# Sorting the experts ahead of the first unit, an earlier sum and an earlier overflow loop in a decoder layer with 32 experts

## The chip, the cores and the metric

One core of a Trainium2 chip runs the whole layer as one program. The metric is the device time of one execution in microseconds (us). A run is timed three times, and one more execution is recorded by the hardware profiler. The engines are named as in the profile: PE is TensorE, DVE is VectorE, ACT is ScalarE, POOL is GpSimd and SP is SyncE, which here issues the weight loads.

## The reference

One layer for one sequence of 512 tokens and a model width of 1024, in float32. A first half mixes tokens (HGRN2 and NSA attention). The second half, which the change touches, is a mixture of 32 experts: each token goes to its top 2 experts inside one group, each expert is a SwiGLU of width 512, and the two outputs are added with weights. A residual sum and a layer norm close the layer. Cut to that half:

```python
def _hier_moe(h, ...):
    ...
    comb = grp_p * jax.nn.softmax(top_l, axis=-1)
    expert = grp_idx * EXP_PER_GROUP + top_i
    ...
    order = jnp.argsort(e_flat)
    ...
    def expert_block(args):
        xb, e = args
        return (jax.nn.silu(xb @ w1[e]) * (xb @ w3[e])) @ w2[e]
    ...
    y = y_pad[dest] * w_s[:, None].astype(x.dtype)
    out = jnp.zeros_like(x).at[tok_s].add(y)

# in reference():
        y = (1 + g2[:, None]) * _hier_moe(h, ...)
        x = _layer_norm(ALPHA * x + y) * ln2_g[l] + ln2_b[l]
```

## The kernel before, in words

The program is written by hand as one list of instructions for each engine; an engine runs its list in order, and semaphores make it wait for the others. So the order of the code is the order on each engine.

The expert half works through 13 *units* (`units = [-2, -1] + ORDER`). A unit is 128 rows of gathered tokens, split among 1 expert of 128 rows, 2 of 64 or 4 of 32. Units -2 and -1 are the experts 0 to 3, which are known ahead of time. The other experts are ranked by their number of tokens, and a unit takes experts by rank: `sort_experts` counts the tokens (four matmuls on PE into `pcnt`), ranks the experts and works out each token's place on DVE, and leaves the order as integers in `ovi`. SP reads expert numbers from `ovi` (`ev`) to address the loads of the units after -1.

For each unit the code does, in this order: `weighted` (DVE: one-hot rows of the unit's tokens times their weights, `pw`); `up` (PE: the products p1 and p3 with exp_w1 and exp_w3; ACT: silu of p1; DVE: `s = silu(p1) * p3`); the loads of the next unit (`load_unit`, SP, tiles `ew` of 512 KB each, three matrices of four tiles for each expert); `combine` of the *previous* unit, whose weighted halves `yh` and `yl` are spread to the tokens by one-hot matmuls (PE, into `pcb`) and added to `acc` (DVE); for every second unit `gather` (PE, `pgx`) of the tokens of the next two; and `down` (PE: transposes `pat` and `ptw`, product `py` with exp_w2; DVE and ACT: `pT`, `y`, `yh`, `yl`). `todo` keeps what `combine` needs one unit later.

The weight tiles come from a ring of 36 buffers (`Q`), 24 of which are free for weights, so a load waits until PE has read the tile that was in its buffer. Other scratch of half that size comes from a ring of 24 buffers (`S`), PSUM from a ring of 8 (`PS`).

The last unit is taken apart. Its exp_w2 is loaded in quarters of 256 columns, its `down` is done by quarter (`quarter_up`, `quarter_y`), and `quarter_add` adds, for each quarter and each 128 tokens, the second to last unit's two terms and the last unit's two terms in one PSUM sum, and adds that to `acc` with a row sum for the norm. Ahead of the last quarter's sums stands `overflow()`, a loop over blocks of tokens beyond a unit's room; its number of turns is read at run time, and it is nought in the profiled execution. The four 128-row pieces are then normed and stored.

Of the kernel before, what the change touches and what calls it, by code (L numbers as in the profile page):

```python
# [21 lines left out]
F32 = mybir.dt.float32  # L22
F32R = mybir.dt.float32r
BF = mybir.dt.bfloat16
# [7 lines left out]
NT = T // 128  # L32
# [109 lines left out]
def hybrid_kernel(ctx, tc, a, out, dbg=None, stop=None):  # L142
# [17 lines left out]
    def S(name, dt=F32):  # L160
        return big.tile([128, 512], dt, name=name, tag="S", bufs=24)
# [1209 lines left out]
    def sort_experts():  # L1371

        pcnt = PS("pcnt")
        for j in range(NT):
            mm(pcnt[:, 0:32], onesb, mb[:, j, :], j == 0, j == NT - 1)
        srt = S("srt")
        key, rk, base, cap_, t6, cnt = (srt[:, 32 * j:32 * j + 32] for j in range(6))
        V.tensor_copy(cnt, pcnt[:, 0:32])
        V.scalar_tensor_tensor(key, cnt, 32.0, iota[:, 0:32], op0=OP.mult, op1=OP.subtract)
        V.tensor_scalar(key[:, 0:4], iota[:, 0:4], -1.0, -100.0, op0=OP.mult, op1=OP.add)  # L1380
        big2 = S("cmpm").bitcast(BF).rearrange("p (e f) -> p e f", e=32)
        V.tensor_tensor(big2, key[:, None, :].to_broadcast([128, 32, 32]),
                        key.rearrange("p (e o) -> p e o", o=1).to_broadcast([128, 32, 32]), op=OP.is_gt)
        V.tensor_reduce(rk.rearrange("p (e o) -> p e o", o=1), big2, axis=AX.X, op=OP.add)

        V.tensor_tensor(big2, rk[:, None, :].to_broadcast([128, 32, 32]),
                        iota[:, 0:32].rearrange("p (e o) -> p e o", o=1).to_broadcast([128, 32, 32]), op=OP.is_equal)
        V.tensor_tensor(big2, big2, iota[:, None, 0:32].to_broadcast([128, 32, 32]), op=OP.mult)
        V.tensor_reduce(ovf[:, 0:32].rearrange("p (j o) -> p j o", o=1), big2, axis=AX.X, op=OP.add)
        V.tensor_copy(ovi[:, 0:32], ovf[:, 0:32])  # L1390
        t1 = S("t1")[:, :256].rearrange("p (c i e) -> p c i e", c=2, i=NT)

        def look(dst, table):

            V.tensor_tensor(t1, oh2, table[:, None, None, :].to_broadcast([128, 2, NT, 32]), op=OP.mult)
            V.tensor_reduce(dst.rearrange("p c (i o) -> p c i o", o=1), t1, axis=AX.X, op=OP.add)

        V.tensor_scalar(cap_, rk, 2.0, 64.0, op0=OP.is_lt, op1=OP.mult)
        V.tensor_scalar(t6, rk, 12.0, 32.0, op0=OP.is_lt, op1=OP.mult)
        V.tensor_add(cap_, cap_, t6)
        V.tensor_scalar(t6, rk, 28.0, 32.0, op0=OP.is_ge, op1=OP.mult)
        V.scalar_tensor_tensor(cap_, cap_, 32.0, t6, op0=OP.add, op1=OP.add)
        V.tensor_scalar(base, rk, 64.0, 128.0, op0=OP.mult, op1=OP.add)
        V.scalar_tensor_tensor(base, rk, 128.0, base, op0=OP.mult, op1=OP.min)
        V.tensor_scalar(t6, rk, 32.0, 512.0, op0=OP.mult, op1=OP.add)
        V.tensor_tensor(base, base, t6, op=OP.min)
        look(bst, base)  # L1410
        look(capt, cap_)
        V.tensor_tensor(far, pos, capt, op=OP.is_ge)
        V.tensor_add(slots, bst, pos)
        V.scalar_tensor_tensor(slots, far, 1e5, slots, op0=OP.mult, op1=OP.add)
        probe("slots", slots)


        ov = S("ov")
        need, incl, st0, t5 = ov[:, 0:32], ov[:, 32:64], ov[:, 64:96], ov[:, 96:128]
        V.tensor_sub(t5, cnt, cap_)  # L1420
        V.tensor_scalar(need, t5, 0.0, None, op0=OP.is_gt)
        for j in range(1, 4):
            V.scalar_tensor_tensor(need, t5, 128.0 * j, need, op0=OP.is_gt, op1=OP.add)
        V.tensor_tensor_scan(incl, need, need, 0.0, OP.add, OP.max)
        V.tensor_sub(st0, incl, need)
        look(ob, st0)
        V.scalar_tensor_tensor(oslots, ob, 128.0, pos, op0=OP.mult, op1=OP.add)
        V.tensor_sub(oslots, oslots, capt)
        V.tensor_scalar(far, far, 1e5, -1e5, op0=OP.mult, op1=OP.add)
        V.tensor_add(oslots, oslots, far)  # L1430
        le = S("le").bitcast(BF)[:, 0:NOV * 32].rearrange("p (j e) -> p j e", j=NOV)
        V.tensor_tensor(le, incl[:, None, :].to_broadcast([128, NOV, 32]),
                        iota[:, 0:NOV].rearrange("p (j o) -> p j o", o=1).to_broadcast([128, NOV, 32]), op=OP.is_le)
        V.tensor_copy(ovf[:, 32:33], incl[:, 31:32])
        V.tensor_reduce(ovf[:, 33:33 + NOV].rearrange("p (j o) -> p j o", o=1), le, axis=AX.X, op=OP.add)
        V.tensor_copy(ovi[:, 32:33 + NOV], ovf[:, 32:33 + NOV])
# [21 lines left out]
        t = w[k // 2]  # L1458
        return t[k % 2] if isinstance(t, list) else t[:, (k % 2) * 512:(k % 2 + 1) * 512]

    def up(xe, n0, ws, rhs=k1):
        lhs = lambda k: xe[k // 2][:, k % 2, :]
        p1 = PS("p1")
        unit_mm(p1, lhs, n0, ws["exp_w1"], rhs, 8)
        s1 = S("s1")
        A.activation(s1, p1, AF.Silu)
        p3 = PS("p3")
        unit_mm(p3, lhs, n0, ws["exp_w3"], rhs, 8)
        V.tensor_mul(s1, s1, p3)  # L1469
        return s1  # L1470
# [50 lines left out]
    def overflow():  # L1521
        ocnt = cp.tile([128, 1], F32, name="ocnt")
        V.memset(ocnt, 0.0)
        nonlocal S
        S, s_ring = (lambda name, dt=F32: Q(name, dt)[:, 0:512]), S
        with tc.For_i(0, nblk, 1) as jb:
            ex = nc.sync.value_load(ovi[0:1, ds(jb + 33, 1)], min_val=0, max_val=NE - 1)
            rel = rel_to(oslots, ocnt)
            V.tensor_scalar(ocnt, ocnt, 128.0, None, op0=OP.add)
            pw = weighted(rel)  # L1530
            xe = gather(one_hots([rel]))

            ow = [S("ow") for _ in range(2)]

            def stream(name):

                def get(k):
                    w = ow[k % 2]
                    nc.sync.dma_start(w, expert_rows(name, ex)[:, k * 512:(k + 1) * 512])
                    return w  # L1540
                return get
            act = up(xe, 0, {n: [stream(n)] for n in ("exp_w1", "exp_w3")}, lambda w, k: w(k))
            combine(*down(act, {"exp_w2": [stream("exp_w2")]}, pw, lambda w, h: w(h)))

            for i in range(NT):
                V.tensor_reduce(sums[:, i, 0:3], acc[i][:, 0:768].rearrange("p (q n) -> p q n", q=3), axis=AX.X, op=OP.add)
                squares(i, 0)
        S = s_ring


    units = [-2, -1] + ORDER
    todo, hots, nblk = None, None, None
    ws = w_first
    for n, u in enumerate(units):
        pw = weighted(rels.pop(u))
        nxt = units[n + 1:n + 3] if n % 2 == 1 else []
        if nxt:
            for x in nxt:
                rels[x] = rel_to(slots, 128.0 * x)
            hots = one_hots([rels[x] for x in nxt])  # L1560
        if n == 4:

            nblk = nc.values_load_multi_w_load_instructions(
                ovi[0:1, 32:33], min_val=0, max_val=NOV - 1,
                skip_runtime_bounds_check_because="a sum of fewer blocks than NOV")[1][0]
        act = up(xe, (n % 2) * 128, ws)
        if n == 0:
            sort_experts()
        w_now = ws
        if n + 1 < len(units):  # L1570
            v_ = units[n + 1]
            if v_ < 0:
                es = (2, 3)
            elif v_ < 2:
                es = (ev(v_),)
            elif v_ < 7:
                es = (ev(2 * v_ - 2), ev(2 * v_ - 1))
            else:
                es = tuple(ev(4 * v_ - 16 + x) for x in range(4))
            ws = load_unit(es, quarters=n + 2 == len(units))  # L1580
        if todo is not None and n + 1 < len(units):
            combine(*todo)
        if nxt:
            xe = gather(hots)
        if n + 1 < len(units):
            todo = down(act, w_now, pw)
    l2g = row_bc("l2g", a["ln2_g"])
    l2b = row_bc("l2b", a["ln2_b"])

# [22 lines left out]

    def quarter_add(q, y, i):

        o = q % 2 * 256
        terms = [(todo[0], t[:, o:o + 256]) for t in todo[1][q // 2]] + [(pT, t) for t in y]
        pc_ = PS("pcb")[:, 0:256]
        for j, (p_, t) in enumerate(terms):
            mm(pc_, p_[:, i * 128:(i + 1) * 128], t, j == 0, j == 3)
        z = acc[i][:, q * 256:(q + 1) * 256]  # L1620
        V.tensor_tensor_reduce(out=z, in0=z, in1=pc_, scale=1.0, scalar=0.0, op0=OP.add, op1=OP.add,  # L1621
                               accum_out=sums[:, i, q:q + 1])
# [35 lines left out]
            V.tensor_scalar(nsh, sums[:, :, 0], -1.0 / 256, None, op0=OP.mult)  # L1658
    squares(2, 0)
    squares(3, 0)  # L1660
    overflow()
    A.preload_act_table_set("natural_log_exp_and_others")
    V.tensor_reduce(l3[:, :, 4:5], sums[:, :, 0:3], axis=AX.X, op=OP.add)
    for i in range(NT):
# [42 lines left out]
```

## Time and profile before

| what | value |
|---|---|
| time, median of 3 runs | 1278.86 us (1274.62 to 1282.39) |
| time of the profiled execution | 1276.27 us |
| span of the profiled execution | 1274.4 us |
| PE busy | 1176.6 us, 92% of the span |
| DVE, ACT, POOL busy | 697.5, 425.5, 123.4 us |
| mean granted clock of PE | 0.98 |
| bytes moved by the DMA queues | 297.15 MB, mean 233 GB/s |

Busy time is the sum over an engine's instructions, and a PE that is busy is not PE at its peak. The time of the profiled execution stands beside its span, which goes from the first to the last instruction; the difference of 1.9 us lies around it. In the trace a tile's name comes without its number, so `p` is p1 or p3, `s` the product s, `ew` any expert weight tile. Line L182 is a helper that issues most matmuls, L184 the same helper where a product uses part of PE's columns.

### The profile page before, as it was taken

What the parts mean: (1) busy time and instruction counts of PE and PEld (TensorE: products, weight loads), DVE (VectorE), ACT (ScalarE), POOL (GpSimd) and SP (SyncE); (2) the same over time, 40 slices, a digit from 0 to 9 for tenths busy, and PEclk for the clock granted to TensorE, in tenths of its full rate; (3) what the DMA queues carried; (4) which work ended last, traced back from release to release, by engine and by line L of the source; (5) the groups of instructions that cost most, each with busy time, mean ns of one, the idle gap of its engine ahead of it and who ended that gap; (6) DMA issues with size and microseconds to landing.
All of it is one profiled execution on the core that took longest, in us unless ns stands there. A gap on an engine that the chain in (4) does not pass through costs nothing. (4 is left out here: it accounts for less than half of the span.)

```text
span 1274.4 us, 18563 instructions
## 1 busy us (share of the span) xinstructions
PE 1176.6 (92%) x6663; PEld 813.2 (64%) x6663; DVE 697.5 (55%) x1621; ACT 425.5 (33%) x897; POOL 123.4 (10%) x179
## 2 busy tenths in 40 slices
PE   5999999999999999999979969999999899899993
PEld 4788898778888888878758953525335235143442
DVE  5564988887565665314596786534143143313436
ACT  5233666664536254554131421201102012010113
POOL 3011111111110011010250140000000000000002
PEclk9999999999999999999999979999999999999997
DMA  9954413324334153345425279799999999999991
GB/s 324 295 152 139 120 52 117 104 87 129 112 109 142 45 174 100 92 147 156 132 66 182 79 301 361 297 411 408 409 409 409 409 409 408 409 409 407 403 346 68
DMA packets 140863, 297.15 MB, mean 233 GB/s; under 512 B 11099, under 2 KB 82979, under 8 KB 140768
## 3 DMA queue, kind: packets, MB, share of 16 engines
q1 hardware_dynamic: 131296, 268.57, 57.5%
q0 software_dynamic: 8704, 25.00, 6.2%
q10 hardware_dynamic: 768, 2.37, 0.5%
q8 instruction: 53, 0.87, 0.3%
q14 instruction: 42, 0.34, 0.1%
HBM read 293.76 MB, written 4.76 MB: 234 GB/s over the span
## 5 line engine op out<-in xcount | busy, mean ns | idle before, releaser
L184 PE MATMUL p<-ew,xe 128*32 128x512 f32 (+1 forms) x960 | 209.0, 599 | 14.9 <-DMA ew<-in_exp_w_dram 14.4
L277 DVE TENSOR_TENSOR wl<-wst,wh 128x1024 fp32r<-128x1024 f32 (+1 forms) x93 | 124.2, 1365 | 75.1 <-ACT wh L276 74.4
L184 PEld LDWEIGHTS p<-ew,xe 128*32 128x32 f32 (+1 forms) x960 | 55.1, 122 | 166.7 <-DMA ew<-in_exp_w_dram 85.4
L184 PE MATMUL py<-ew,aT 128*32 128x512 f32 (+2 forms) x496 | 96.6, 570 | 7.8 <-DMA ew<-in_exp_w_dram 5.2
L276 ACT ACTIVATE wh<-wst 128x1024 fp32r<-128x1024 f32 (+1 forms) x94 | 93.0, 1030 | 29.5 <-POOL wst L275 16.6
L1469 DVE TENSOR_TENSOR s<-s,p 128x512 f32<-128x512 f32 x13 | 8.9, 687 | 142.3 <-PE p L184 136.4
L184 PEld LDWEIGHTS py<-ew,aT 128*32 128x32 f32 (+1 forms) x496 | 27.1, 122 | 70.5 <-issue 34.2
L1490 DVE SCALAR_TENSOR_TENSOR y<-py,cs,g2b 128x512 f32<-128x512 f32 (+1 forms) x28 | 19.9, 710 | 85.5 <-PE py L184 75.4
L1492 ACT ACTIVATE yh<-y 128x512 fp32r<-128x512 f32 (+1 forms) x28 | 16.8, 599 | 139.4 <-DVE y L1490 132.8
L1355 ACT ACTIVATE xe<-pgx,sm 128x256 f32<-128x256 f32 (+1 forms) x48 | 26.3, 547 | 106.2 <-PE pgx L182 106.2
L182 PE MATMUL pgx<-pm,xhh 128*128 128x256 f32 (+1 forms) x224 | 58.3, 299 | 1.5 <-DVE pm L1242 1.5
L182 PE MATMUL pgx<-pm,xhl 128*128 128x256 f32 (+1 forms) x224 | 57.6, 296 | 0.0
L1516 DVE TENSOR_TENSOR acc<-acc,pcb 128x512 f32<-128x512 f32 x88 | 53.5, 679 | 0.0
L515 POOL DMA_DIRECT2D adaw<-in_ada_w_dram x64 | 34.5, 541 | 196.0 <-PE ptp L188 42.0
L182 PE MATMUL pmg<-hh,wh 128*128 128x512 f32 x128 | 50.4, 394 | 0.0
L182 PE MATMUL psg<-hh,wh 128*128 128x512 f32 x128 | 50.3, 393 | 0.0
L182 PE MATMUL psg<-hl,wh 128*128 128x512 f32 x128 | 49.9, 390 | 0.0
L182 PE MATMUL pmg<-hh,wl 128*128 128x512 f32 x128 | 49.9, 390 | 0.0
L182 PE MATMUL psg<-hh,wl 128*128 128x512 f32 x128 | 49.9, 390 | 0.0
L182 PE MATMUL pmg<-hl,wh 128*128 128x512 f32 x128 | 49.8, 389 | 0.0
L182 PE MATMUL pcb<-yh,pT 128*128 128x512 f32 (+1 forms) x120 | 44.5, 381 | 5.1 <-DVE s L1469 2.9
L182 PEld LDWEIGHTS pgx<-pm,xhh 128*128 128x128 f32 x224 | 46.1, 206 | 2.6 <-DVE pm L1242 1.9
(513 smaller groups left out, 2843.0 us busy)
## 6 DMA issues: line engine op xcount, KB each, us to landing
ew<-in_exp_w_dram SPq DMA_DIRECT2D x380, 512.0 KB, 10.1
wst<-in_w_in_dram SPq DMA_DIRECT2D x66, 512.0 KB, 4.8
adaw<-in_ada_w_dram POOLq DMA_DIRECT2D x64, 256.0 KB, 3.1
adaw<-in_ada_w_dram SPq DMA_DIRECT2D x16, 512.0 KB, 9.2
wst<-in_w_br_hg_dram SPq DMA_DIRECT2D x8, 512.0 KB, 3.8
wst<-in_w_br_nsa_dram SPq DMA_DIRECT2D x8, 512.0 KB, 4.5
wst<-in_w_out_dram SPq DMA_DIRECT2D x8, 512.0 KB, 4.9
ext_d<-ext_d POOLq DMA_DIRECT2D x1, 2560.0 KB, 17.3
```

Of the source, the lines that this page charges most:

```text
L182: PE.matmul(o, l, r, start=start, stop=stop)
L184: PE.matmul(o, l, r, start=start, stop=stop, tile_position=pos)
L276: A.activation(wh, self.w[j], AF.Copy)
L277: (sub or V).tensor_sub(wl, self.w[j], wh.bitcast(F32))
L515: P_.dma_start(w, ada[:, k, 2048 + j * 512:2560 + j * 512])
L1355: A.activation(xe[k // 2][:, k % 2, 0:128 * u], pgx, AF.Identity, bias=sm2[:, 0, k:k + 1], scale=sm2[:, 1, k:k + 1])
L1469: V.tensor_mul(s1, s1, p3)
L1490: V.scalar_tensor_tensor(y, py, cs_, g2b[c0 // 512][:, c0 % 512:c0 % 512 + n], op0=OP.mult, op1=OP.mult)
L1492: A.activation(yh, y, AF.Copy)
L1516: V.tensor_add(acc[i][:, s_], acc[i][:, s_], pc_)
```

## The change

Three things move. `sort_experts()` is called ahead of the loop over the units, where it stood behind the first unit's `up`. In the last unit, `combine` of the second to last unit is called inside `up`, between its two products, and `quarter_add` keeps two of its four terms. `overflow()` is called right behind the loop over units, ahead of the loads of ln2_g and ln2_b and of the last `down`; its body no longer makes the row sums and squares, and most of its scratch comes from the S ring again. The sort's scratch shares tiles that had names of their own.

```diff
-        key, rk, base, cap_, t6, cnt = (srt[:, 32 * j:32 * j + 32] for j in range(6))
+        key, rk, base, cap_, t6, cnt, need, incl, st0, t5 = (srt[:, 32 * j:32 * j + 32] for j in range(10))
...
-        ov = S("ov")
-        need, incl, st0, t5 = ov[:, 0:32], ov[:, 32:64], ov[:, 64:96], ov[:, 96:128]
...
-        le = S("le").bitcast(BF)[:, 0:NOV * 32].rearrange("p (j e) -> p j e", j=NOV)
+        le = cmpm[:, 0:NOV * 32].rearrange("p (j e) -> p j e", j=NOV)
...
-    def up(xe, n0, ws, rhs=k1):
+    def up(xe, n0, ws, rhs=k1, mid=None):
...
         A.activation(s1, p1, AF.Silu)
+        if mid:
+            mid()
         p3 = PS("p3")
...
-        S, s_ring = (lambda name, dt=F32: Q(name, dt)[:, 0:512]), S
+        S, s_ring = (lambda name, dt=F32: Q(name, dt)[:, 0:512] if name in ("ow", "xe", "pm") else s_ring(name, dt)), S
...
-
-            for i in range(NT):
-                V.tensor_reduce(sums[:, i, 0:3], acc[i][:, 0:768].rearrange("p (q n) -> p q n", q=3), axis=AX.X, op=OP.add)
-                squares(i, 0)
...
     ws = w_first
+    sort_experts()
     for n, u in enumerate(units):
+        last = n + 1 == len(units)
...
-        act = up(xe, (n % 2) * 128, ws)
-        if n == 0:
-            sort_experts()
+
+        act = up(xe, (n % 2) * 128, ws, mid=(lambda: combine(*todo)) if last else None)
...
-        if todo is not None and n + 1 < len(units):
+        if todo is not None and not last:
             combine(*todo)
...
+    overflow()
     l2g = row_bc("l2g", a["ln2_g"])
     l2b = row_bc("l2b", a["ln2_b"])
...
-        o = q % 2 * 256
-        terms = [(todo[0], t[:, o:o + 256]) for t in todo[1][q // 2]] + [(pT, t) for t in y]
         pc_ = PS("pcb")[:, 0:256]
-        for j, (p_, t) in enumerate(terms):
-            mm(pc_, p_[:, i * 128:(i + 1) * 128], t, j == 0, j == 3)
+        for j, t in enumerate(y):
+            mm(pc_, pT[:, i * 128:(i + 1) * 128], t, j == 0, j == 1)
...
     squares(3, 0)
-    overflow()
```

On DVE, at the first unit, before the change: the last row of `weighted` (pw, tw), the product s, and behind it the first rows of the sort.

```order
L1444 TENSOR_SCALAR pw<-cst,rel,cw 128x128
L1445 TENSOR_SCALAR tw<-cst,rel,cw 128x128
L1446 TENSOR_TENSOR pw<-pw,tw 128x512
L1469 TENSOR_TENSOR s_7413<-s_7413,p_7415 128x512
L1378 COPY srt<-pcnt 128x32
L1379 SCALAR_TENSOR_TENSOR srt<-srt,cst 128x32
```

The same place with the change: the last rows of the sort, the whole of `weighted`, the product s and what follows it.

```order
L1434 TENSOR_REDUCE ovf<-cmpm 128x20
L1435 CAST ovi<-ovf 128x21
L1443 TENSOR_SCALAR pw<-cst,rel,cw 128x128
L1444 TENSOR_SCALAR tw<-cst,rel,cw 128x128
...
L1445 TENSOR_TENSOR pw<-pw,tw 128x512
L1470 TENSOR_TENSOR s_7463<-s_7463,p_7465 128x512
```

The line of dots stands for the same two rows three times more. The whole sort and `weighted` have come to stand ahead of s; behind s, where the sort stood, the first unit's pT follows.

On POOL, at the end of the program, one piece of the difference: the loads of ln2_g and ln2_b (l2g, l2b), and the branches of the overflow loop (L1526 before, L1527 now).

```order
+L1527 COMPARE_AND_BRANCH
+L1527 UNCONDITIONAL_BRANCH x2
+L1699 BRANCH_PREFETCH_HINT
+L1527 REGISTER_ALU
+L1527 COMPARE_AND_BRANCH
+L1527 UNCONDITIONAL_BRANCH
 L974 DMA l2g<-in_ln_g_dram 128x1024
 L974 DMA l2b<-in_ln_b_dram 128x1024
-L1526 COMPARE_AND_BRANCH
-L1526 UNCONDITIONAL_BRANCH x2
-L1703 BRANCH_PREFETCH_HINT
```

The loop has moved from behind the two loads to ahead of them.

On PE, in the last unit with the change: the end of `combine` of the second to last unit, the product p3, and the loop's entry with the first matmul of its body.

```order
L182 MATMUL pcb<-yh,pT 128x512
L182 MATMUL pcb<-yl,pT 128x512
L184 MATMUL p_10770<-ew,xe 64x512 x16
L1527 COMPARE_AND_BRANCH
L1527 UNCONDITIONAL_BRANCH x2
L1699 BRANCH_PREFETCH_HINT
L182 MATMUL pgx<-pm,xhh 128x128
```

Before, the two products of the last unit stood next to each other, pat followed them, and the loop's entry stood behind the third quarter's sums.

## Rows read from the trace of the kernel before

**Rows 1.** Windows of the expert stage: busy us of PE, PEld, DVE, ACT, POOL; PEclk, DMA share, GB/s

```profile
757.50:766.50 9.00, 8.52 (x42) 6.45 (x43) 5.53 (x25) 2.36 (x6) 0.00 (x0) 0.65 0.03 10
766.50:813.00 46.50, 42.58 (x206) 19.24 (x203) 34.26 (x95) 6.15 (x11) 0.00 (x0) 0.96 1.01 393
813.00:822.00 9.00, 8.75 (x62) 6.43 (x63) 0.69 (x1) 4.26 (x9) 0.00 (x0) 1.00 0.25 81
829.00:1224.00 395.00, 372.17 (x1800) 156.61 (x1794) 138.58 (x315) 51.97 (x100) 1.14 (x2) 1.00 1.03 408
1232.00:1241.00 9.00, 7.90 (x52) 4.17 (x51) 2.71 (x5) 1.59 (x4) 0.00 (x0) 1.00 0.92 292
```

**Rows 2.** Waits of SP's queue, 740 to 830 us: total, times, longest

```profile
SPq L1270 <- PE py L184: 20.7, 7, 13.4
SPq L1270 <- PE p L184: 19.3, 9, 14.8
```

**Rows 3.** Timeline of PE, first two units: start us, us, [idle before <-releaser]

```profile
764.04 13.95 PE L184 MATMUL p<-ew,xe 128*64 128x512 f32 x64
...
778.88 0.75 PE L188 MATMUL pat<-cst,s 128*128 128x128 f32 x4 [0.69 <-DVE s L1469]
...
787.29 13.90 PE L184 MATMUL p<-ew,xe 128*64 128x512 f32 x64
...
807.52 0.50 PE L182 MATMUL pcb<-yh,pT 128*128 128x512 f32 x1 [2.93 <-DVE s L1469]
...
818.72 3.65 PE L184 MATMUL py<-ew,aT 128*64 128x512 f32 x16 [0.25 <-ACT aT L1477]
```

**Rows 4.** Timeline of DVE, first unit: weighted, s, and the sort's first and last row

```profile
766.59 0.35 DVE L1444 TENSOR_SCALAR pw<-cst,rel,cw 128x128 f32<-128x128 f32 x1
...
778.14 0.69 DVE L1469 TENSOR_TENSOR s<-s,p 128x512 f32<-128x512 f32 x1 [8.68 <-PE p L184]
778.75 0.18 DVE L1378 COPY srt<-pcnt 128x32 f32<-128x32 f32 x1
...
794.34 0.18 DVE L1436 CAST ovi<-ovf 128x21 int32<-128x21 f32 x1
```

**Rows 5.** Window behind PE's wait at 804.6 us, columns as in rows 1

```profile
808.20:811.60 3.40, 3.40 (x17) 3.40 (x17) 3.40 (x7) 0.56 (x1) 0.00 (x0) 0.50 1.04 414
```

**Rows 6.** Timeline of PE, last unit

```profile
1219.79 14.78 PE L184 MATMUL p<-ew,xe 128*64 128x512 f32 x64
...
1235.42 0.75 PE L188 MATMUL pat<-cst,s 128*128 128x128 f32 x4 [0.85 <-DVE s L1469]
...
1242.56 1.95 PE L184 MATMUL py<-ew,aT 128*64 128x256 f32 x16
...
1246.54 1.95 PE L184 MATMUL py<-ew,aT 128*64 128x256 f32 x16
...
1252.75 0.39 PE L182 MATMUL pcb<-yh,pT 128*128 128x256 f32 x1 [2.15 <-issue]
```

**Rows 7.** The loop's line: ns min/median/max; then a wait of SP's queue

```profile
L1526 PEldq EVENT_SEMAPHORE  x13: 51/51/51, 1250.6 to 1252.4; - x13
...
L1526 PEldq COMPARE_BRANCH  x3: 101/187/319, 1248.5 to 1252.5; - x3
...
SPq L1526 <- SPq L1526: 6.9, 5, 1.5
```

**Rows 8.** Quarter loads: issue, landing; POOL's queue, 1220 to 1245 us: packets, MB, share

```profile
L1267 SPq DMA_DIRECT2D ew<-in_exp_w_dram x8: 543/1158/5980, 1220.4 to 1235.8; - x8
...
DMA to landing us min/median/max: 8.2/8.9/13.8
...
q0 software_dynamic: 288, 1.05, 10.8%
```

**Rows 9.** Timelines of ACT and DVE behind the loop: table load, first norm scale

```profile
1252.37 1.28 ACT L1662 ACT_TABLE_LOAD   x1 [1.34 <-DVEq L1526]
...
1256.30 0.16 DVE L1625 SCALAR_TENSOR_TENSOR l<-sqs,l 128x2 f32<-128x2 f32 x1
```

More of the change, by code (lines that the diff above doesn't have):

```diff
@@ L1380, in sort_experts @@
         V.tensor_scalar(key[:, 0:4], iota[:, 0:4], -1.0, -100.0, op0=OP.mult, op1=OP.add)
-        big2 = S("cmpm").bitcast(BF).rearrange("p (e f) -> p e f", e=32)
+        cmpm = S("cmpm").bitcast(BF)
+        big2 = cmpm.rearrange("p (e f) -> p e f", e=32)
         V.tensor_tensor(big2, key[:, None, :].to_broadcast([128, 32, 32]),
@@ L1584, in hybrid_kernel @@
             xe = gather(hots)
-        if n + 1 < len(units):
+        if not last:
             todo = down(act, w_now, pw)
+    overflow()
     l2g = row_bc("l2g", a["ln2_g"])
```

## The prediction

> **What bounds the kernel now.** I read the windows table of the expert stage first. Once the weights stream, from 829 to 1224 us, the DMA engines are full (share 1.03, 408 GB/s) and every other engine has slack [rows 1]. So in this stretch nothing is won or lost by compute: its length is the bytes divided by that rate. What the change can move is the point at which the full stretch begins, and what comes after the last weight has landed. The reader should see three places in that table: a hole before 766.5 us (10 GB/s), a full stretch to 813, and a second hole from 813 to 822 us (81 GB/s). Then come 395 full microseconds, and an end where quarter-wide loads run at only 292 GB/s.
>
> Next I asked what the DMA queue of SyncE waited for between 740 and 830 us. Its longest waits are single ones on TensorE (PE): 14.8 us for the first unit's up product (p) and 13.4 us for a down product (py) [rows 2]. Both are buffer waits: the next weight tile needs a tile that PE is still to read. The 13.4 us end about 2 us after the second unit's down product starts at 818.72 us [rows 3]. That product restarts the stream, and the whole rest of the kernel is queued behind it. **Each microsecond that it comes later is a microsecond of the total.**
>
> **The sort, moved ahead of the first unit.** On PE it is four tiny matmuls, 0.3 us, which it keeps. On VectorE (DVE) the block runs from 778.75 to 794.52 us: 15.8 us [rows 4]. Today it stands after the first unit's product s = silu(p1)*p3, so PE's next steps (pat, py, the second unit's up product) run beside it [rows 3]. DVE itself sits idle 8.68 us ahead of s [rows 4], which looks like room for the sort; it is too small. After the change DVE starts the sort where `weighted` starts now, at 766.6, ends it at 782.4, then does `weighted` (766.59 to 769.46, 2.9 us) until 785.3, and s is done at 786.0 in place of 778.83. PE's pat waits for s: it starts **7.2 us late**. Queued behind pat on PE are the first down product, the second unit's up product and, in the end, the py that restarts the stream.
>
> Three things change that figure. First, PE is idle for 7.8 us ahead of pat. The trace has a smaller case: idle 2.93 us ahead of 807.52, and the granted clock of the next 3.4 us was 0.50, that is 1.2 instead of 2.4 GHz [rows 3, 5]. I take 5 us at half clock after the longer wait, which costs 2.5 us; the bounds are nothing and 4 us. Second, that 2.93 us wait itself goes away. There PE's eighth combine pair waited for the second unit's s, which DVE reached late because the sort had pushed everything behind it back; with the sort out of the way DVE is waiting for p3 instead. Third, the 1.7 us lost in that half-clock stretch goes too. Sum at the restart: 7.2 + 2.5 - 2.9 - 1.7 = **+5.1 us**, between +2.6 (clock stays up) and +7. A new DMA hole about 792 to 797 us, because the first down product frees its tiles later, is inside this: those loads are done by 823.5, just before the restart at 823.8.
>
> The register loads of expert numbers need only the sort's first half; SyncE reaches them after the first down product, so an earlier sort gives them nothing.
>
> **The sum of the second to last unit, moved into the last up product.** Sixteen 128x512 matmuls and eight DVE adds go between p1 and p3. Seven such pairs took 3.4 us of PE today (801.19 to 804.59, that is the end of p to the start of the wait) [rows 3], so eight take 3.9. The last p takes 14.78 us against 13.95 for the first [rows 3, 6]: 0.8 us of it is waiting for weights, which the combine fills. The up product ends at about 1237.5 in place of 1234.57, and s at 1238.3. By itself that is +3 us, but the next edit covers it.
>
> **The overflow loop, ahead of the last down product.** Its body doesn't run in this profile, yet it isn't free: all engines meet at it. SyncE alone waited 6.9 us in five steps of up to 1.5 us there, on its own queue [rows 7]; these are landings. The last quarter tile is issued at 1235.8 and the shortest landing takes 8.2 us [rows 8], so the last weight is in at 1244.0. Today the loop stands ahead of the fourth quarter's sums, and by then the loads have long landed. After the change pat, aT and all four quarters of the down product stand behind it, so the first quarter can't start on its own weights any more: it waits for the last ones. On ScalarE, aT, and on DVE, pT and y are queued there too.
>
> When is the last landing? The two rows ln2_g and ln2_b now stand behind the loop on GpSimd. Today they take 10.8% of the 16 DMA engines over 25 us amid the quarter loads [rows 8], 2.7 us; I take 2.5 of it as given back, landing at **1241.5**. Each engine polls 13 semaphores [rows 7]; some five remain after the last landing, and with the branch PE goes on some 0.9 us later, at 1242.4. pat starts there in place of 1235.42 [rows 6]: **+7.0 us**. Bounds: 1241.3 (all given back, one poll) and 1244.9 (nothing given back), +5.9 to +9.5. The rows themselves need a few us from about 1243 and are used after 1257: covered.
>
> What the tail gets back. Between the third and fourth quarters' products PE has 3.98 us per quarter, of which 1.95 is the product itself [rows 6]; the sixteen matmuls of a sum take the other 2. Eight remain, so each of the sums is 1 us shorter. The loop's 2.15 us hole ahead of the fourth sum [rows 6] closes. Following pat to the first norm scale, today 1235.42 to 1256.30 = 20.9 us [rows 6, 9]: the third quarter's product starts at +6.1 (was +7.1), the fourth at +9.1 (was +11.1), the fourth sums at +12.5 (was +17.3), the last DVE add ends at +15.3 (was +20.0). But the table load on ScalarE (1.28 us) [rows 9], today inside the loop's hole, then stands ahead of the last squares, so the norm is at +17.1: **-3.8 us**. PE was idle 5 us before pat; at half clock for another 5 us the dense products lose **+2.4** (bounds 0 and 4). Sum at the end: 7.0 - 3.8 + 2.4 = **+5.6 us**, between +2 and +9.7. Renaming the sort's scratch tiles, and the S tiles inside the loop body, add no instruction that runs: zero.
>
> **Sum.** +5.1 + 5.6 = +10.7 us. On the profiled execution's 1276.27 us (span 1274.4) that is 1287.0. The three timed runs had a median of 1278.86, 2.6 above it; on that footing I predict **1289.6**, +0.84%.
>
> A page's rule speaks against the price of the loop. The Trainium skill (Advanced Engine Details and Errata, Control Flow Timing) gives some 51 ns for a branch and 108 ns for a compare and branch. PE's three branches of this loop took 101 to 319 ns [rows 7], which agrees for a branch, but the waits beside them are what costs. If the loop were its branches alone, the end would come out as rival 2 says.
>
> **Rivals.**
> 1. *The clock stays up in both places.* For it: PE's 2.15 us idle at 1250 left it up. Against: 2.93 us idle at 804.6 did not [rows 3, 5], and both new waits are longer. Then 2.6 + 3.2 = +5.8 us: 1284.7.
> 2. *The loop costs its branches alone.* pat then starts after s, at 1238.6: +3.2 - 3.8 = -0.6 at the end, in all +4.5: 1283.4. Against it stand SyncE's landings at the loop [rows 7].
> 3. *The sort fits.* The other side, not slower. Were s not late, the restart would gain the 2.9 + 1.7 = 4.6 us that today's late combine costs, and against +5.6 at the end leave +1.0: 1279.9. It decides at s: the start breaks even when s is at most 4.6 us late with the clock up, that is a sort of 13.2 us or less; a gain of all 4.6 us needs one that ends by 775. For it stands the 8.68 us hole; against it the block's 15.8 us.
> 4. *Worse.* Nothing given back by ln2_g and ln2_b, and the clock low for longer: +15 or more, 1294 to 1296.
>
> **How the numbers follow.** Forecast (both places lose, +8 to +14 us) 0.52; rival 1 0.19; rival 2 0.09; rival 3 0.08; rival 4 0.12. The range takes the sums' ends, +2 to +18, without the outermost parts: **1281 to 1297**; only rival 3 and stray runs fall out. Half a per cent, 6.4 us, is about what a measurement of this kernel can tell from no change. Rivals 1 and 2 lie close under that line; with the forecast and rival 4 above it, half of rival 1 and a third of rival 2: slower 0.75; same 0.2; faster 0.05, for a place where both ends lose less than their lower bounds.
>
> **What would show it.** After: the sort's first row on DVE at about 766.6 and s some 7 us later than now; PE idle before the first pat, released by DVE; a py wait of SyncE that ends near 825.8; a last tile that lands 5 us later minus 2.5. At the end PE idle about 5 us ahead of the last pat, with nothing but the loop to release it, and half clock behind it; quarter sums of eight matmuls. Wrong if pat of the first unit isn't late, if the DMA stretch after it begins no later, or if the last pat starts right after s.

## The result and the profile after

The changed kernel takes 1286.99 us (median of 9 runs, 1282.87 to 1290.23), against 1277.90 us for the kernel before (9 runs, 1274.62 to 1282.39). The ratio is 1.0069, with a 95% interval of 1.0049 to 1.0090: slower by 6 to 11.5 us. The profiled execution took 1282.87 us, the shortest of the nine; its span is 1281.1 us, 6.7 us more than before.

The two traces must be laid over each other at a common row. The first unit's p, ahead of which the change moves only the sort's four tiny matmuls, starts at 762.98 us here and at 764.04 before; over all traces of this study that row lies between 762.98 and 766.24. So places below are counted from that row of the same trace.

Windows of the expert stage, columns as in rows 1:

```profile
766.50:785.00 18.50, 10.80 (x52) 3.64 (x49) 17.08 (x49) 0.60 (x1) 0.00 (x0) 0.89 0.99 379
786.00:792.00 6.00, 6.00 (x27) 2.01 (x27) 0.69 (x1) 1.08 (x3) 0.00 (x0) 0.84 0.36 145
792.00:797.00 5.00, 5.00 (x26) 1.67 (x24) 2.10 (x3) 1.26 (x2) 0.00 (x0) 1.00 0.66 229
820.00:824.00 4.00, 3.75 (x21) 1.46 (x21) 0.69 (x1) 1.26 (x4) 0.00 (x0) 1.00 0.34 114
829.00:1224.00 395.00, 371.61 (x1810) 156.47 (x1804) 138.23 (x313) 51.99 (x100) 0.00 (x0) 1.00 1.03 408
```

The long stretch is the same 408 GB/s as before [rows 1]. The hole that lay at 813 to 822 us has become two: the stream thins out from 786 to 797 us (145, then 229 GB/s), where the prediction put a new hole at 792 to 797, and again behind 820 (114 GB/s), where it waits for the second unit's py as before.

SyncE's waits, 740 to 830 us, then PE's and DVE's timelines of the first two units:

```profile
SPq L1270 <- PE py L184: 23.7, 7, 11.9
SPq L1270 <- PE p L184: 19.5, 9, 13.4
```

The 11.9 us are now the wait for the first unit's py, in the first hole.

```profile
762.98 13.95 PE L184 MATMUL p<-ew,xe 128*64 128x512 f32 x64
784.63 1.13 PE L188 MATMUL pat<-cst,s 128*128 128x128 f32 x4 [7.70 <-DVE s L1470]
...
794.13 13.90 PE L184 MATMUL p<-ew,xe 128*64 128x512 f32 x64
807.96 0.50 PE L182 MATMUL pcb<-yh,pT 128*128 128x512 f32 x1
...
820.74 7.09 PE L184 MATMUL py<-ew,aT 128*64 128x512 f32 x32 [0.25 <-ACT aT L1478]
```

```profile
765.36 0.19 DVE L1378 COPY srt<-pcnt 128x32 f32<-128x32 f32 x1
...
781.02 0.18 DVE L1435 CAST ovi<-ovf 128x21 int32<-128x21 f32 x1
781.11 0.34 DVE L1443 TENSOR_SCALAR pw<-cst,rel,cw 128x128 f32<-128x128 f32 x1
...
783.89 0.68 DVE L1470 TENSOR_TENSOR s<-s,p 128x512 f32<-128x512 f32 x1
```

On DVE the sort, `weighted` and s follow one another without a gap: s no longer waits for p, as it did for 8.68 us [rows 4], but PE's pat waits for s. PE stands still for 7.70 us ahead of pat. What comes back is seen at 807.96: the combine runs through without the 2.93 us wait of rows 3. SyncE's wait for py ends at 822.70 us, 59.7 us behind p; before it was 56.6.

The granted clock behind PE's two long waits, the later one first (columns as above; the clock is the third number from the end):

```profile
1246.00:1250.00 4.00, 4.00 (x26) 2.38 (x26) 1.04 (x2) 1.17 (x3) 0.28 (x1) 0.66 0.80 251
782.00:786.00 4.00, 1.37 (x7) 1.38 (x8) 2.54 (x7) 0.21 (x1) 0.00 (x0) 0.50 1.02 409
786.00:790.00 4.00, 4.00 (x17) 1.44 (x17) 0.69 (x1) 1.08 (x3) 0.00 (x0) 0.76 0.54 217
```

At 782 us it is 0.50 (1.2 in place of 2.4 GHz), and the window means of 0.76 and 0.66 are mixtures of the two levels.

Then the last unit, on PE and DVE:

```profile
1222.23 7.04 PE L184 MATMUL p<-ew,xe 128*64 128x512 f32 x32
...
1233.05 7.09 PE L184 MATMUL p<-ew,xe 128*64 128x512 f32 x32
1244.92 0.93 PE L188 MATMUL pat<-cst,s 128*128 128x128 f32 x4 [4.78 <-SPq L1527]
...
1252.40 1.95 PE L184 MATMUL py<-ew,aT 128*64 128x256 f32 x16
...
1255.41 1.95 PE L184 MATMUL py<-ew,aT 128*64 128x256 f32 x16
```

```profile
1240.26 0.69 DVE L1470 TENSOR_TENSOR s<-s,p 128x512 f32<-128x512 f32 x1 [5.42 <-PEq L1527]
...
1262.91 0.17 DVE L1622 SCALAR_TENSOR_TENSOR l<-sqs,l 128x2 f32<-128x2 f32 x1 [0.21 <-ACT sq L1599]
```

s is ready at 1240.95, and pat starts 4 us later: its releaser is SyncE at the loop's line. What SyncE does there, and the quarter loads:

```profile
SPq L1527 <- SPq L1527: 6.8, 5, 1.5
```

```profile
L1267 SPq DMA_DIRECT2D ew<-in_exp_w_dram x8: 543/1147/3127, 1222.9 to 1235.8; - x8
...
DMA to landing us min/median/max: 8.1/9.3/11.4
```

```profile
L1527 PEldq COMPARE_BRANCH  x3: 97/179/310, 1235.8 to 1244.7; - x3
```

The last quarter tile is issued at 1235.8 and lands some 8.1 us later (the shortest landing); SyncE's wait for it ends at 1244.01, and pat follows 0.9 us behind. The third and fourth quarters' products now start 3.01 us apart, in place of 3.98 [rows 6].

### The profile page after: what moved, and what is told of

It reads as the page before. It is cut to its first block, busy times and chain, and to the rows that moved or that the text cites. A ratio compares the mean times of both kernels' runs of the same rounds, so it can differ in the third digit from the quotient of the medians.

```text
span 1281.1 us, 18536 instructions
## 1 busy us (share of the span) xinstructions
PE 1175.4 (92%) x6647; PEld 811.0 (63%) x6647; DVE 702.4 (55%) x1629; ACT 426.1 (33%) x897; POOL 124.0 (10%) x179
## 5 line engine op out<-in xcount | busy, mean ns | idle before, releaser
L1517 DVE TENSOR_TENSOR acc<-acc,pcb 128x512 f32<-128x512 f32 x96 | 58.4, 681 | 1.3 <-PE pcb L182 1.3
L182 PE MATMUL pgx<-pm,xhh 128*128 128x256 f32 (+1 forms) x224 | 55.4, 288 | 1.5 <-DVE pm L1242 1.5
L182 PE MATMUL pgx<-pm,xhl 128*128 128x256 f32 (+1 forms) x224 | 55.0, 287 | 0.0
L1478 ACT ACTIVATE aT<-pat 128x512 f32<-128x512 f32 x13 | 7.8, 597 | 114.4 <-PE pat L188 114.4
## 6 DMA issues: line engine op xcount, KB each, us to landing
ew<-in_exp_w_dram SPq DMA_DIRECT2D x380, 512.0 KB, 10.1
```

The source lines that it names most:

```text
L182: PE.matmul(o, l, r, start=start, stop=stop)
L1478: A.activation(aT, at_.rearrange("p (f s) -> p f s", f=4), AF.Copy)
L1517: V.tensor_add(acc[i][:, s_], acc[i][:, s_], pc_)
```

## The experiments

Names that begin with a are the changed kernel with one thing altered, those with b the kernel before. The table gives places of each trace in us: first p as it stands, then, counted from it, the first pat, py of unit -1, the first quarter load's issue, the last pat and the first norm scale (DVE's `l<-sqs,l` of 128x2). Two columns are stretches: from the first pat to the next p, and from the last pat to the first quarter sum, which tell what the clock takes. The ratio is to runs of the kernel before taken beside each row's own, so the ratios, and not the medians, are the ones to compare.

```
kernel         first p  pat    to p    py     load    last pat  to sum  norm    median   ratio (95%)
before          764.04  14.84   8.40  54.67  456.37   471.38    5.04   492.26  1277.90
after           762.98  21.65   9.51  57.76  459.89   481.94    6.34   499.93  1286.99  1.0069 (1.0049, 1.0090)
a_sort_back     766.07  15.22   8.35  55.05  457.05   479.07    6.04   496.76  1281.60  1.0026 (1.0014, 1.0039)
a_loop_back     766.22  21.62   9.43  57.65  459.10   477.25    5.04   495.89  1286.95  1.0062 (1.0042, 1.0082)
a_loop_back2    763.48  21.63  10.05  58.32  459.87   477.94    5.04   496.43  1282.31  1.0045 (1.0030, 1.0061)
a_rows_ahead    763.91  21.63  10.34  58.62  460.33   484.73    7.57   503.96  1287.99  1.0081 (1.0061, 1.0100)
a_no_loop       765.03  21.62   9.39  57.63  459.97   477.12    5.04   493.82  1279.48  1.0009 (0.9997, 1.0021)
a_fill          765.86  21.66   8.35  56.62  458.43   482.42    5.04   499.11  1285.38  1.0043 (1.0027, 1.0058)
b_sort_ahead    766.21  21.63  11.00  59.23  461.11   476.12    5.04   496.99  1281.91  1.0024 (1.0012, 1.0035)
b_mid           766.24  14.84   8.40  54.68  456.68   474.81    5.04   493.30  1278.99  1.0005 (0.9991, 1.0020)
b_split_sort    764.40  14.84   8.40  49.85  451.37   466.33    5.04   488.06  1273.38  0.9969 (0.9958, 0.9981)
b_down_first    765.70  14.84   8.40  45.40  457.19   472.15    5.04   493.03  1278.02  0.9999 (0.9985, 1.0013)
b_split_down    765.95  14.84   8.40  39.46  451.11   466.01    5.04   487.62  1271.73  0.9961 (0.9946, 0.9976)
b_split_late    766.13  15.25   8.40  39.87  449.35   464.35    5.04   486.46  1270.71  0.9929 (0.9915, 0.9943)
```

**The sort undone, and the sort alone.** The first puts the call back:

```diff
-    sort_experts()
     for n, u in enumerate(units):
...
         act = up(...)
+        if n == 0:
+            sort_experts()
```

> The changed kernel with the sort alone back behind the first unit's up product. Theory (the sort on DVE makes s late, and the restart of the weight stream with it): in the changed kernel's trace, counted from the start of the first unit's p, s came 6.8 us later than before, the two units after it lost 1.1 us of clock, and 4.8 us of PE's wait in the combine went away, net +3.1 us. So py of unit -1 returns to 54.7 us after p's start (57.8 in the changed kernel), PE's wait for s inside the combine is back with about 2.9 us, and the whole is 3 us shorter than the changed kernel (about 1284). Rival (the sort fits, the loss is all at the end): no change against the changed kernel, 1287.

The second makes the opposite edit in the kernel before.

> The kernel before with the first edit alone, the sort called ahead of the loop over the units. Theory (by the traces so far): py of unit -1 starts 57.7 us behind the first p in place of 54.7, the first quarter load is issued 3.0 to 3.5 us later counted from the same row, and the time is 3 to 3.5 us longer than before, about 1281. The timed runs of the changed kernel with and without the sort's move differ by 5.4 us; if that is the price, 1283. Rival (the sort costs only together with the loop's move): no change, 1278.

PE in the first run's combine:

```profile
809.92 0.50 PE L182 MATMUL pcb<-yh,pT 128*128 128x512 f32 x1 [2.97 <-DVE s L1470]
```

Both theories hold in their mechanism. Without the sort's move py is back at 55.05 us and PE waits 2.97 us for s in the combine. With the sort's move alone py is at 59.23, 1.5 us later than the 57.7 expected, since the clock took 2.6 us in that trace (11.00 against 8.40). The medians say 5.4 us less, and 3.6 us more than the 1278.28 of the runs beside it; the intervals of the ratios (1.0026 against 1.0069, and 1.0024 against 1) leave 1.5 to 4.5 us for the second and wider bounds for the first. The traces say 2.7 to 4.7 us at py and at the norm. The rival, that the sort costs nothing by itself, is out.

**The loop put back ahead of the last sums.** There were two tries. In the first the loop stood too late, behind the early table load. Both also put the row sums and the scratch of the loop's body back as they were before; the body doesn't run.

```diff
-    overflow()
     l2g = row_bc("l2g", a["ln2_g"])
...
     squares(3, 0)
     A.preload_act_table_set("natural_log_exp_and_others")
...
+    overflow()
     for i in range(NT):
         quarter_add(3, y, i)
```

> The changed kernel with the overflow loop alone back ahead of the last quarter's sums; the loads of ln2_g and ln2_b stay ahead of the last down product, as before. Theory (the loop makes the last down product wait for the last weight's landing): the last pat follows s at once, 3.9 us earlier than in the changed kernel, the half clock behind it goes (1 us), the loop's hole ahead of the last sums returns (2.2 us on PE, partly beside DVE's work), and the two rows take 2.5 us of the quarter loads again, which no longer matters: 3 to 4 us shorter than the changed kernel, about 1283.5. Rival (the loop costs its branches alone): under 1 us either way, 1286 to 1288.

This was a miss, with no gain in time (1.0062 against 1.0069). Yet pat came 4.7 us earlier (477.25) and the first norm scale 4.0. Behind that row the program takes 22.6 us to its end, against 18.2 in the changed kernel, and ScalarE and DVE show why:

```profile
1258.50 1.28 ACT L1601 ACT_TABLE_LOAD   x1
...
1261.90 1.28 ACT L1625 ACT_TABLE_LOAD   x1
...
1263.51 1.28 ACT L1626 ACT_TABLE_LOAD   x1
```

```profile
1265.05 0.16 DVE L1627 SCALAR_TENSOR_TENSOR l<-l 128x2 f32<-128x2 f32 x1 [2.77 <-ACT l L1626]
```

Behind the loop this program loads a table at each change of function: six loads in the tail in place of one, and DVE waits 2.77 and then 2.96 us in place of 0.60 each time. The likely reason, which no run isolates, is that the loop's body uses another function on ScalarE, although the body never ran; that the loop's place behind the early load brings the six loads is shown by the next run.

The second try moves that line up by three:

```diff
     squares(3, 0)
+    overflow()
     A.preload_act_table_set("natural_log_exp_and_others")
...
-    overflow()
     for i in range(NT):
```

> As the run before with the loop back, but with the loop ahead of ScalarE's early table load, as in the kernel before; in the first try it stood behind it, and ScalarE then loaded five tables of 1.28 us in the tail in place of one. Theory: that trace had the first norm scale 495.9 us behind the first unit's p, against 499.9 in the changed kernel, and lost the 4 us again to four table loads; without them the whole is 3.5 to 4.5 us shorter than the changed kernel, about 1283. Rival (the loop costs its branches alone): 1286 to 1288.

With the loop ahead of the table load there is one load again, and the theory holds in the trace: the norm is at 496.43, 3.5 us earlier than in the changed kernel. The median is 4.7 us shorter (1282.31), but the intervals of the two ratios overlap. PE has its hole again:

```profile
1255.90 0.39 PE L182 MATMUL pcb<-yh,pT 128*128 128x256 f32 x1 [2.18 <-DVEq L1527]
```

**No loop at all.**

```diff
-    overflow()
     l2g = row_bc("l2g", a["ln2_g"])
```

> The changed kernel without the overflow loop, which leaves out the blocks of tokens beyond a unit's room (none in this data). It measures the loop's whole price where the change has put it. Theory (a barrier that waits for the last landing): the last pat starts 0.9 us or less behind s, at about 1241 in place of 1244.9, PE's clock stays up behind it (1 us more), and the rows ahead take 2.5 us of the quarter loads, which the later quarters' products may feel by up to 1 us: 4 to 5.5 us shorter than the changed kernel, about 1282. Rival (branches alone): 1 us shorter at most.

```profile
1242.15 0.75 PE L188 MATMUL pat<-cst,s 128*128 128x128 f32 x4 [0.86 <-DVE s L1470]
```

pat follows s, the clock stays up, and the norm comes 6.1 us earlier (499.93 to 493.82); by the medians 7.5 us, more than the 4 to 5.5 expected. So a loop that turns no time costs 6.1 us ahead of the last down product, 4.8 of them pat's later start and 1.3 the clock behind it, and 2.6 us (496.43 to 493.82) where it stood before. The 6.1 us hold with the two rows of the norm loaded behind the loop; with the rows ahead of it, the next run, it is 10.1 (503.96, of which 0.4 lies ahead of the first quarter load). The Trainium skill (Advanced Engine Details and Errata, Control Flow Timing) gives about 51 ns for a branch and 108 ns for one that compares; PE's three rows took 97 to 310 ns, the shortest near the second figure. Together they are 0.6 of the 6.1 us.

**The rows ahead of the loop.**

```diff
-    overflow()
     l2g = row_bc("l2g", a["ln2_g"])
     l2b = row_bc("l2b", a["ln2_b"])
+    overflow()
```

> The changed kernel with the loads of ln2_g and ln2_b issued ahead of the overflow loop. Theory (the rows took 2.5 us of the DMA engines from the quarter loads, and moving them gave that back): the last weight lands 2.5 us later counted from the first quarter load's issue (23.6 us after it as before, against 21.1 in the changed kernel), the last pat starts 2.5 us later, the whole is 2.5 us longer, about 1289.5. Rival (the landing is set by when PE frees the quarter tiles' buffers, as the fourth quarter tile's issue ended at 1230.58 us before and 1230.19 in the changed kernel): landing and time as in the changed kernel, 1287.

```profile
L1267 SPq DMA_DIRECT2D ew<-in_exp_w_dram x8: 542/1148/5988, 1224.2 to 1239.6; - x8
...
DMA to landing us min/median/max: 8.2/8.8/13.8
```

```profile
1248.64 1.13 PE L188 MATMUL pat<-cst,s 128*128 128x128 f32 x4 [7.16 <-SPq L1527]
```

The last landing comes 23.6 us behind the first quarter load's issue (1239.6 + 8.2 - 1224.2), as before the change; with the rows behind the loop it was 21.1. pat follows it at 0.8 us. So landing and pat move together, and the buffers' rival is out. The rows are 1.05 MB [rows 8], an estimated 2.6 us at the stream's 408 GB/s, which fits. The longer wait (7.16 us) also costs more clock: 7.57 us to the first sum, against 6.34. The norm comes 4.0 us later; the timed runs (+1.0 us in the median, the intervals overlap) can't tell that from none.

**The second to last unit's sum alone**, in the kernel before.

```diff
-        act = up(xe, (n % 2) * 128, ws)
+        act = up(xe, (n % 2) * 128, ws, mid=(lambda: combine(*todo)) if n + 1 == len(units) else None)
...
-        terms = [(todo[0], t[:, o:o + 256]) for t in todo[1][q // 2]] + [(pT, t) for t in y]
+        terms = [(pT, t) for t in y]
```

> The kernel before with the second edit alone: the second to last unit's combine inside the last up product, quarter sums of two terms, the loop and the two rows left where they were. Theory (PE does the same work in both places): the last up ends 3.1 us later, each of the four quarter sums is 1 us shorter, but the last one is hidden in part beside DVE, so the first norm scale comes 0 to 1 us later: 1278.4 to 1279.4, no change that can be measured. Rival 1 (all of the combine stays on the path): +3, 1281.4. Rival 2 (each shorter sum counts and the combine fills waits for weights): -2, 1276.4.

The last pat is 3.4 us later, the norm 1.0 us, and the time is the same within its interval (0.9991 to 1.0020, that is -1.2 to +2.6 us). The theory holds; the interval leaves out both rivals, the first narrowly.

**PE kept busy.** Matmuls on data at hand, with a result that nobody reads, fill the two waits:

```diff
+    def fill(n):
+        o = PS("fill")
+        for _ in range(n):
+            mm(o, xhh[0][:, 0:128], xhh[0][:, 0:512], True, True)
...
         act = up(...)
+        if n == 0:
+            fill(31)
...
+    fill(19)
     overflow()
```

> The changed kernel with idle time of PE filled by matmuls whose result nobody reads: 31 (7.1 us) ahead of the first unit's pat, 19 (4.4 us) ahead of the overflow loop. Theory (the half clock behind PE's two long waits costs 1.1 to 1.9 us at the first unit and 1.0 to 1.3 at the last): the granted clock stays at 1.00 behind both waits, pat to the next p takes 8.4 us in place of 9.5 to 10.3, pat to the first quarter sum 5.1 in place of 6.3, and the whole is 2 to 3 us shorter than the changed kernel, 1284 to 1285. Rival (the clock's price is hidden behind the DMA stream): the rows shorten, the time stays at 1287. A third: PE reaches the loop late through the filling, and the time is longer.

```profile
782.00:786.00 4.00, 4.00 (x20) 3.30 (x18) 3.93 (x15) 0.00 (x0) 0.00 (x0) 1.00 1.03 415
```

```profile
1241.47 4.60 PE L182 MATMUL fill<-xhh 128*128 128x512 f32 x19
1248.28 0.75 PE L188 MATMUL pat<-cst,s 128*128 128x128 f32 x4 [2.21 <-issue]
```

The clock stays at 1.00, and both stretches are back at 8.35 and 5.04 us: the clock's price in the changed kernel's trace is 1.1 and 1.3 us. At the end the third expectation came in as well: PE reached the loop at 1246.07, behind the last landing (1245.37), and pat started 2.2 us behind PE's arrival in place of 0.9 us behind the landing. The whole is 0.8 us shorter by the norm, and 1.6 us by the medians, but the intervals of the two ratios overlap, so the 2 to 3 us expected are not shown.

**A sort cut in two.** The same idea, made to fit DVE's wait:

```diff
     def sort_experts():
...
         V.tensor_copy(ovi[:, 0:32], ovf[:, 0:32])
+        yield
...
+        if n == 0:
+            sorting = sort_experts()
+            next(sorting)
         act = up(xe, (n % 2) * 128, ws)
         if n == 0:
-            sort_experts()
+            next(sorting, None)
```

> The kernel before with the sort cut in two: its first part, up to the ranks and their integers (7 us on DVE), goes behind weighted and ahead of the first unit's up product, the rest stays behind it. Theory: the first part fits into DVE's 8.7 us of waiting ahead of s, so s isn't late (under 0.5 us), DVE is 7 us earlier behind it, PE's wait of 2.9 us for the second unit's s and the half clock behind it (1.7 us) go, py of unit -1 starts 50 us after the first p in place of 54.7, and the whole is 4.6 us shorter than before: 1273.8. Rival 1 (the restart is set by the DMA queue, not by PE): no change. Rival 2 (s is late anyway): +2 or more.

```profile
776.62 0.18 DVE L1390 CAST ovi<-ovf 128x32 int32<-128x32 f32 x1
778.50 0.69 DVE L1470 TENSOR_TENSOR s<-s,p 128x512 f32<-128x512 f32 x1 [1.71 <-PE p L184]
```

The theory holds. The first part ends with 1.7 us to spare, s and pat are not late (14.84 both times), the combine no longer waits, and py comes 4.8 us earlier. The time is 0.9969 of before (0.9958 to 0.9981).

**The second unit's down ahead of combine and gather**, alone and with the cut sort:

```diff
+        if n == 1:
+            prev, todo = todo, down(act, w_now, pw)
+            combine(*prev)
-        if todo is not None and n + 1 < len(units):
+        elif todo is not None and n + 1 < len(units):
             combine(*todo)
...
-        if n + 1 < len(units):
+        if n != 1 and n + 1 < len(units):
             todo = down(act, w_now, pw)
```

> The kernel before with only the second unit's down put ahead of combine and gather; the sort is where it was. Theory (py of unit -1 frees the tiles on which the stream's restart waits): py starts about 45 us behind the first p in place of 54.7 (it still waits for the late s), the hole of 7 us in the stream shrinks as in the run with the sort cut in two as well, and the whole is 3.5 to 5 us shorter than before, about 1273.5. Rival (the sort's lateness, not the order of down, sets the gain): under 2 us.

> The same with one more edit: at the second unit, down stands ahead of combine and gather, so its product py, which frees the weight tiles, comes some 9 us earlier still. Theory: the hole in the DMA stream about 813 to 822 us (7 us of full rate lost in the profile of before) closes, and the whole is 7 us shorter than before, 1271.4; the gain ends there because the stream is full. Rival 1 (the hole opens again later, since the next tiles are freed only by the third unit's p behind combine and gather): 3 to 5 us of the 7, about 1274. Rival 2 (the start of the stream doesn't set the end): no change.

In the last version the passed combine is put off by a unit as well:

```diff
             prev, todo = todo, down(act, w_now, pw)
-            combine(*prev)
         elif todo is not None and n + 1 < len(units):
+            if n == 2:
+                combine(*prev)
             combine(*todo)
```

> The faster version (sort cut in two, down ahead of combine and gather at the second unit) with the combine that it passes put off by one unit, so that the third unit's p starts 3.8 us earlier. Theory: the rest of the hole, about 1 us of full rate near 826 to 831 us, closes: 0.5 to 1.2 us shorter than that version, 1270.5 to 1271. Rival: nothing more is gained since another wait stands behind it, 1271.7.

PE of the first of the three, then the windows 822 to 831 of the first and 827 to 831 of the second, and 813 to 831 of the third:

```profile
809.19 1.13 PE L188 MATMUL pat<-cst,s 128*128 128x128 f32 x4 [6.34 <-DVE s L1469]
...
831.78 13.10 PE L184 MATMUL p<-ew,xe 128*32 128x512 f32 x114
```

```profile
822.00:831.00 9.00, 8.78 (x67) 8.15 (x66) 8.22 (x18) 4.00 (x8) 0.00 (x0) 1.00 0.58 234
```

```profile
827.00:831.00 4.00, 4.00 (x40) 1.17 (x36) 0.00 (x0) 0.00 (x0) 0.00 (x0) 1.00 0.80 249
```

```profile
813.00:822.00 9.00, 9.00 (x78) 8.14 (x80) 4.85 (x13) 5.34 (x10) 0.00 (x0) 1.00 1.03 410
822.00:831.00 9.00, 9.00 (x86) 2.70 (x79) 0.00 (x0) 0.60 (x1) 0.00 (x0) 1.00 1.02 407
```

The first was a miss: py did come at 45.4 us as the theory said, yet nothing was gained. PE now waits 6.34 us for the late s with nothing beside it, since the combine that filled that time stands behind. The rival holds: with s late, the order of down gains nothing. The next unit's p starts at 66.1 us (61.7 before), and the hole has moved there (0.58). With the cut sort s is on time and py comes at 39.5 us, but a thinner hole opens at 827 (0.80), so that little is won over the cut sort alone (1271.73 against 1273.38; rival 1 of that run). With the combine put off as well there is no hole left: 410 and 407 GB/s through. That version takes 1270.71 us, 0.9929 of before (0.9915 to 0.9943), and is the fastest of all. Over the second version it gains 1.8 us at the first quarter load (451.11 to 449.35) and 1.2 at the norm. The medians say 1.0 us; the ratios, each to its own runs of the kernel before, say about 4 us, and their intervals do not touch. That it is faster is shown; by how much stays open.

## Why the prediction was right, step by step

The forecast was 1289.6 us and +0.84%; measured are 1286.99 and +0.69%. It was reached by the way described, with both losses somewhat smaller. The total came within 2.6 us, nearer than the terms did in the traces, which give +7.7 us against +10.7 said. How much of that nearness is luck stays open, as the part on the clock says.

**s late.** Said 7.2 us for pat, measured 6.81 (14.84 to 21.65); the sort's first row stands 2.4 us behind the first p, said 2.6 (766.6 less 764.0).

**The wait that goes.** Said 2.9 and 1.7 us, together 4.6; from the second p to py it is 31.43 before and 26.60 after: 4.83.

**The clock behind the first wait.** Said 2.5, bounds 0 and 4; measured 1.11 in this trace (8.40 to 9.51). This is the term that was mis-sized, and with the two above it makes the restart +3.1 in place of +5.1: SyncE's wait ends 59.7 us behind the first p, and not 61.8 (825.8 less 764.0). The same code gave 1.0 to 2.6 us over the six traces with the early sort that have no filling, so the value taken was one that occurs, only not here. The filled run shows that it is the clock. The trace is also of the shortest of the nine runs, with the highest mean granted clock (0.978, against 0.972 to 0.974 in the seven longest), so the usual run may have lost more; where it did, no trace shows.

**The last landing.** The two rows were to give back 2.5 us: 23.6 to 21.1, so 2.5. Counted from the first p the last landing is 1.0 us late, 3.5 from the stream less 2.5; the run with the rows ahead of the loop takes it away again.

**pat behind the loop.** Said +7.0 us with 0.9 us from landing to pat. From the first quarter load's issue to pat it is 15.01 us before and 22.05 after: +7.0; the 0.9 was measured too. The rows-ahead run shows the cause, since pat moved with the landing. The 13 polls of rows 7 are PE's; SyncE has 21 at that line, so "each engine" was not right, though nothing in the sum hangs on it.

**The tail.** Said -3.8 and +2.4 for the clock. From pat to the first norm scale it is 20.88 and 17.99, with 1.30 for the clock: -4.2 and +1.3.

**The sum.** The stream's first quarter load is 3.5 us late, the end adds 4.15 (7.0 - 4.2 + 1.3): 7.7 us at the first norm scale, against +10.7 said. The medians say 9.1, with 6 to 11.5 left open.

**The bounds.** The prediction's own sums give 7.2 + 4 - 2.9 - 1.7 = 6.6 for the upper end of the restart, where it says 7. With both ends they span about +5 to +16 us, so the range of +2 to +18 was wider than the sums, and not narrower as it says. The measured change lies inside either.

**One way only.** "Each microsecond that it comes later is a microsecond of the total" held for delays, and for the cut sort's 4.8 us. It does not hold for py alone: put ahead of combine and gather it came 9.3 us earlier, and the time stayed, because the stream then waited for the third unit's p.

**The rivals.** The clock did not stay up (0.50 and 0.66). The loop costs more than its branches (6.1 us). The whole sort does not fit. That rival's figure, 4.6 us to be had where the sort ends in time, was right: the cut sort got 4.8 at py.

What stays open is the rest between traces and timed runs: single traces differ by up to 3.3 us before the change begins and by 1.6 us in the clock's price behind the first wait, so terms below 1 us are read from stretches within a trace and not from the times.

## What to carry to other kernels

A kernel that is bound by a stream still has places where compute sets it: find the wait on which the stream restarts, and ask of each edit whether it delays the engine that ends that wait. Work that is moved into an engine's idle time must be shorter than that time (15.8 us into 8.7 lost 2.7 to 4.7 us, 7.2 of them won 4.8), and when one hole is closed the next must be looked for, as it may open one product later. The run-time loop of this kernel turns no time and is still a meeting of the engines and the outstanding transfers: such a loop belongs where the last transfer has landed already (2.6 us in place of 6.1), with the early table load behind it.

## What was not expected of the hardware

The clock's price behind the first pat's wait of 7.2 to 7.7 us was not the same in each trace: 9.39, 9.43, 9.51, 10.05, 10.34 and 11.00 us for one and the same stretch, against 8.40 at full clock. In the first try with the loop put back a table load took 1.28 us and its function followed at once (1261.90 to 1263.19 us); the Trainium skill (ScalarE: Activation LUTs, What ACT_TABLE_LOAD costs) gives 1.28 us and a drain of 1.38 for each switch, of which the trace shows the first alone.
